# Which earlier transfers a scatter and a fetch wait for at the end of a one-core transformer kernel, and where the last small unit evicts to

## The chip, the cores and the metric

The kernel runs on one core of a Trainium2 chip. The time is that of one execution on the device, in microseconds (us). The kernel before took 2656.06 us as the median of three runs, 2652.81 us the lowest and 2658.04 us the highest.

Engine names: PE is TensorE (PEld its weight loads), DVE is VectorE, ACT is ScalarE, POOL is GpSimd, SP is SyncE. Each works through its own list of instructions in order. Transfers between the on-chip memory and HBM are started by SP (plain loads and stores) or by POOL (all indirect ones here).

## The reference

Two transformer blocks run on 2048 tokens of width 1024. The second ends in a mixture of experts, and this is where the change lies:

```python
best = argmax(sum of the two best scores of each group)   # 4 groups of 4 experts
idx  = top 2 experts inside the best group
gate = the two scores, divided by their sum
y    = sum over the two experts e of gate * ((silu(x @ w_gate[e]) * (x @ w_up[e])) @ w_down[e])
x    = layer_norm(ALPHA * x + y, ln_moe_g, ln_moe_b)
```

So a token gets two contributions, both from experts of one group, and its last layer norm can be done once that group's experts are through.

## The kernel before

The dense parts take the first 2.2 ms and are the same before and after. They leave every token's row in HBM twice: `x3d` (with its gates) to gather from, and `sumd`, already scaled, to which the experts add.

**Units.** The experts' work is cut into units of 256 tokens (n=2, two tiles of 128) or of 128 (n=1, a third tile of an expert that needs one). There are 23 units, with 39 tiles. The last three, to which the text below refers, are: **U3**, expert 14, two tiles; **U2**, expert 14, its third tile; **U1**, expert 15, two tiles. U4 and U5 stand before these. A unit goes through these steps (class `Unit`):

- `gather`: POOL fetches the tokens' rows from `x3d` by index (L1157), one transfer per tile, into a tile of `XG`.
- `transposed`: PE transposes (L240), ACT and DVE split every number into a high and a low part (L171 and L172), and DVE copies the gate (L1334).
- `up(0)`, `up(1)`: the products with gate and up weights (L181), a half at a time; `act(f)`: ACT takes a tanh (L1205), DVE multiplies (L1206, L1207), ACT and DVE split (L171, L172). A unit with n=1 is transposed once more in `turn` (L1217).
- `down`: the product with the down weights (L181), evicted by ACT with the gate as factor (L1231) into a tile `y`, which POOL scatters into `sumd`, adding to what is there (L1232).

**Last norms.** Tokens are listed by group in 18 tiles of 128: 3, 5, 5 and 3 for the four groups, where the last 3 are the tokens of group 3 without expert 15, and 2 more, called group 4 in the code, for those with expert 15. When a group is done, its tiles are fetched from `sumd` (`fetch`, L1429), their mean and variance taken (`measure`, L1444 and L1445 on DVE, or L1439 and L1440 on ACT; the root on POOL, L190 and L192), normed (`norms`, L1450 and L1451 on DVE) and scattered to the output (L1452).

**Order.** `run` writes the units in a software pipeline: while unit i does its up products, unit i-1 does its down products and unit i+2 gathers. `mids`, `turn`, `late` and `hooks` hang work of the last norms into unit i: `mids` before up(1), `turn` after act(1), `late` after the down products of unit i-1. The order on ACT and DVE is that of the code; PE, POOL and SP are put in order by a scheduler, except that `queued` fixes the order of POOL's transfers and roots among themselves.

**Waits.** `adds` holds the scatters of the latest unit, `reads` the fetches since then. A scatter waits until all of `adds` and `reads` have landed; a fetch waits until the latest `adds` have landed. POOL works in order, so what stands behind a waiting transfer waits too.

**Tiles.** `YT` holds two tiles `y` of 4 KB; a new one waits until the scatter from the one before it in that place has landed. `XG` holds four gather tiles. `FX` holds three tiles of fetched rows; the last fetches use `XG` and `MRAW`.

In the last unit (`else` of `run`) the order is up(0), the down products of U2, `last` (measure, norms, the fetches of group 3), up(1), act(1), and the down products of U1. After it come group 4's two fetches, and the five norms still open.

A loop for experts with more tiles than planned follows (L1520). In the traced execution it is not entered.

Of the kernel before, what the change touches and what calls it, by code (L numbers as in the profile page):

```python
# [20 lines left out]
D = 1024  # L21
# [28 lines left out]
def model(ctx, tc, A, out, taps=None, nsb=NSB, upto=9):  # L50
# [44 lines left out]
    def partition(mem, *kbs):  # L95
        ends = [sum(kbs[:j + 1]) for j in range(len(kbs))]
        return [ring("", kb, mem[:, int((e - kb) * 256):int(e * 256)]) for kb, e in zip(kbs, ends)]
# [9 lines left out]
    def acc(n=512):  # L107
        return turns["acc"]((128, n))
# [74 lines left out]
    def mm3(o, lh, ll, rh, rl, start, stop):  # L183
        mm(o, lh, rh, start, False)
        mm(o, lh, rl, False, False)
        mm(o, ll, rh, False, stop)
# [917 lines left out]
    def moe():  # L1104
# [3 lines left out]
        MRAW, MT, XG, YT, GAINS, FX = partition(work, MR_KB, 7.75, 16.25, 8, 8, 40 - MR_KB)  # L1108
# [10 lines left out]
        adds, reads, outs = [], [], []  # L1119

        def apart(a, b):
            tc.declare_no_dep(a.ins, b.ins, reason="other tokens")

        def after(a, b):
            tc.add_manual_dep(a.ins, b.ins.name, mybir.DependencyInfo(mybir.DependencyClass.Sync,
                                                                      mybir.DependencyReason.DATA), reason="same tokens")

        line = [[], []]

        def queued(*ds_):  # L1130

            if line[0]:
                for d in ds_:
                    for o in line[1]:
                        tc.add_manual_dep(d.ins, o.ins.name, mybir.DependencyInfo(
                            mybir.DependencyClass.NoSync, mybir.DependencyReason.DATA), reason="order")
            line[1] = ds_
            return ds_[0]

        class Unit:  # L1140
# [3 lines left out]
            def __init__(self, load, src_gu, src_d, gate, n, lo=DVE, of=None):  # L1144
                self.lo = lo
                self.of = of
                self.load, self.src_gu, self.src_d, self.gate, self.n = load, src_gu, src_d, gate, n
                self.t, self.a = [], {}
                self.gu, self.dw = (of.gu, of.dw) if of else ([], [])

            def gather(self):
# [68 lines left out]
            def down(self):  # L1220
                new = []
                for r in range(self.n):
                    rs = slice(r * 128, (r + 1) * 128)
                    y = YT((128, D))
                    for hf in range(2):
                        hs = slice(hf * 512, (hf + 1) * 512)
                        a = acc()
                        for f in range(2):
                            h, l = self.dw[f]
                            mm3(a, self.th[:, f, rs], self.tl[:, f, rs], h[:, hs], l[:, hs], f == 0, f == 1)  # L1230
                        ACT.activation(y[:, hs], a, AF.Copy, scale=self.gc[r])  # L1231
                    d = POOL.indirect_dma_start(out=sumd[:, :], out_offset=self.at[r], in_=y, in_offset=None,  # L1232
                                                compute_op=OP.add)
                    for o in new:
                        apart(d, o)
                    for o in adds + reads:
                        after(d, o)
                    new.append(d)
                queued(*new)
                adds[:] = new  # L1240
                reads.clear()

        def run(units, early=None, mids={}, turn={}, late={}, hooks={}):
            n = len(units)
            for j in range(min(2, n)):
                units[j].gather()
            units[0].weights_up(range(4))
            units[0].transposed()
            if early:
                early()  # L1250
            if n > 1:
                units[1].weights_up(range(3))
            for i, u in enumerate(units):
                v = units[i + 1] if i + 1 < n else None
                w = units[i + 2] if i + 2 < n else None
                if w:
                    w.gather()
                u.up(0)
                if i:
                    units[i - 1].weights_down(1)  # L1260
                u.weights_down(0)
                u.act(0)
                if i:
                    units[i - 1].turn()
                if not v:
                    if i:
                        units[i - 1].down()
                    u.weights_down(1)
                if i in mids:
                    mids[i]()  # L1270
                u.up(1)
                u.act(1)
                if v:
                    v.transposed()
                    v.weights_up([3])
                    if i in turn:
                        turn[i]()
                    if i:
                        units[i - 1].down()
                    if i in late:  # L1280
                        late[i]()
                    if w:
                        w.weights_up(range(3))
                    for hook in hooks.get(i, ()):
                        hook()
                else:
                    u.turn()
                    u.down()

# [78 lines left out]
        tabgi = tab[:, 80:80 + NL * 16].bitcast(I32)  # L1368
# [55 lines left out]
            DVE.tensor_copy(tabgi, tabg)  # L1424
            POOL.dma_start(tabgd, tabgi)

        def fetch(at, mem):
            x = mem((128, D))
            d = POOL.indirect_dma_start(out=x, out_offset=None, in_=sumd[:, :], in_offset=at)  # L1429
            for o in adds:  # L1430
                after(d, o)
            reads.append(queued(d))
            return x, at

# [14 lines left out]
        def scaled(x, at, mean, op, r, static=True):  # L1449
            DVE.scalar_tensor_tensor(x, x, mean, gains[:, 0], op0=op, op1=OP.mult)  # L1450
            DVE.scalar_tensor_tensor(x, x, r, gains[:, 1], op0=OP.mult, op1=OP.add)  # L1451
            d = POOL.indirect_dma_start(out=out[:, :], out_offset=at, in_=x, in_offset=None,  # L1452
                                        bounds_check=S - 1, oob_is_err=False)
            for o in outs:
                (apart if static else after)(d, o)
            outs.append(d)
            if static:
                queued(d)
# [6 lines left out]
        ready, got, measured = [], [], []  # L1465

        def group_done(g):
            for c in range(NFIN[g]):
                ready.append(bass.IndirectOffsetOnAxis(ap=tabgi[:, g * 16 + c:g * 16 + c + 1], axis=0))

        def measure():
            while got:
                x, at = got.pop(0)
                measured.append((x, at, *stats(x, DVE)))

        def fetches(n, mem=FX):
            for _ in range(min(n, len(ready))):
                got.append(fetch(ready.pop(0), mem))

        def norms():  # L1480
            while measured:
                scaled(*measured.pop(0))

        units, mids, turn, late, hooks = [], {}, {}, {}, {}
        for e in range(16):
            units.append(static(e, 0, 2))
            if e in (4, 8, 12):
                hooks[len(units) - 1] = [lambda e=e: group_done((e - 1) // 4)]
            if BLOCKS[e] == 3:
                units.append(static(e, 2, 1, units[-1]))  # L1490
# [8 lines left out]

        def last():  # L1500
            measure()
            norms()
            group_done(3)
            fetches(NFIN[3], XG)

        mids[len(units) - 1] = last
        with tc.manual_schedule(engines={getattr(mybir.EngineType, e) for e in MANUAL}):
            line[0] = True
            run(units, None, mids, turn, late, hooks)
            line[0] = False  # L1510
            assert not ready
            group_done(4)
            fetches(NFIN[4], MRAW)
# [6 lines left out]
        with tc.For_i(0, nit) as j:  # L1520
            u = overflow(j)
            run([u])
            finish([fetch(u.at[0], FX)], static=False)
            cv = SP.value_load(ov["gown"][0:1, 1, ds(j, 1)], min_val=0, max_val=NL * 16 - 1)
            ix = sml([128, 1], "ix", I32, bufs=5)
            SP.dma_start(ix, tabgd[:, ds(cv, 1)])
            finish([fetch(bass.IndirectOffsetOnAxis(ap=ix, axis=0), FX)], static=False)
# [12 lines left out]
    if upto >= 4:  # L1540
        moe()
# [87 lines left out]
```

## Time and profile before

| what | us |
|---|---|
| median of three runs | 2656.06 |
| the profiled execution | 2657.26 |
| its span, from the first instruction to the last | 2655.5 |
| PE busy in the span | 2522.8 (95%) |
| DVE busy | 1603.0 (60%) |
| ACT busy | 1119.3 (42%) |
| POOL busy | 565.2 (21%) |
| PE busy from 2300 to 2500 us, the middle of the experts | 197.43 of 200.00 |
| PE busy from 2617.35 us to the end | 0.00 of 38.15 |

All times in the rows below are us from the start of the span. A row of the timeline is one instruction, or a run of like instructions of one engine: its start, its duration, the engine, the line, the operation, what it writes and reads, the shapes and the count; in brackets the idle time of that engine before it and what ended it. For an indirect transfer on POOL the duration is that of starting it, not of moving the data. A row of the waits gives who waited for whom, the total in us, how often, and the longest.

### The profile page before, as it was taken

Reading aid. Unit: us, or ns where it says so; the run is one execution under the profiler, and the core shown is the slowest. Engines: PE = TensorE matmul, PEld = TensorE weight load, DVE = VectorE, ACT = ScalarE, POOL = GpSimd, SP = SyncE. Lnnn points to the kernel's source line nnn. Section 1 sums busy time; section 2 is a strip of 40 time slices with the busy share of each in tenths; the row PEclk is TensorE's granted clock in tenths of the full one; section 3 lists DMA queues with packets and bytes.
Section 4 is the critical chain, followed back from the end, with each engine's and each line's share of the span. In section 5 each row is a group of like instructions: output and inputs, shape, how many; then the busy total and the mean of one; then the engine's idle time right before and its main releaser. Section 6 shows DMA issues by size and latency. Waiting matters only on the chain. (4 is left out here: it accounts for less than half of the span.)

```text
span 2655.5 us, 36764 instructions
## 1 busy us (share of the span) xinstructions
PE 2522.8 (95%) x13870; PEld 2139.3 (81%) x13870; DVE 1603.0 (60%) x3223; ACT 1119.3 (42%) x1994; POOL 565.2 (21%) x616
## 2 busy tenths in 40 slices
PE   8899999999999999999999999999999996999993
PEld 8777888888788888878788878787888786999892
DVE  5536357667563667664646666654476656686774
ACT  5644453343343532433445323344443332555552
POOL 0102202221021032110210411012012222344544
PEclk9999999999999999999999999999999997999996
DMA  8861362345313515442244245412422445799985
GB/s 302 298 222 56 100 199 68 122 141 197 96 57 99 187 48 182 139 155 72 88 150 128 72 163 176 138 48 80 157 82 94 153 149 208 220 281 283 263 246 135
DMA packets 122708, 402.04 MB, mean 151 GB/s; under 512 B 15136, under 2 KB 15280, under 8 KB 122528
## 3 DMA queue, kind: packets, MB, share of 16 engines
q1 hardware_dynamic: 105872, 340.30, 37.8%
q0 software_dynamic: 16656, 59.37, 8.5%
q8 instruction: 109, 1.79, 0.3%
q14 instruction: 71, 0.58, 0.1%
HBM read 320.11 MB, written 80.55 MB: 151 GB/s over the span
## 5 line engine op out<-in xcount | busy, mean ns | idle before, releaser
L181 PE MATMUL bank<-rounded 128*128 128x512 f32 (+2 forms) x10628 | 2175.8, 362 | 36.5 <-ACT rounded L171 25.2
L181 PEld LDWEIGHTS bank<-rounded 128*128 128x128 f32 x10628 | 1761.6, 190 | 337.6 <-ACT rounded L171 29.4
L172 DVE TENSOR_TENSOR rounded<-work,rounded 128x1024 fp32r<-128x1024 f32 (+2 forms) x530 | 580.6, 1108 | 462.7 <-ACT rounded L171 408.0
L171 ACT CAST rounded<-work 128x1024 fp32r<-128x1024 f32 (+3 forms) x552 | 510.7, 941 | 658.4 <-PE bank L181 256.4
L171 ACT CAST rounded<-bank 128x512 fp32r<-128x512 f32 (+1 forms) x220 | 112.3, 554 | 221.4 <-PE bank L240 100.9
L181 PE MATMUL bank<-work 128*128 128x128 f32 (+5 forms) x944 | 163.6, 301 | 6.7 <-DVE work L545 2.1
L181 PEld LDWEIGHTS bank<-work 128*128 128x128 f32 (+1 forms) x944 | 130.7, 190 | 36.5 <-issue 5.1
L172 DVE TENSOR_TENSOR rounded<-bank,rounded 128x512 fp32r<-128x512 f32 (+1 forms) x220 | 133.3, 640 | 41.9 <-ACT rounded L171 40.2
L240 PE MATMUL bank<-ident,work 128*128 128x128 f32 x616 | 86.5, 288 | 27.0 <-DMA work<-x3d,tabi 9.3
L240 PEld LDWEIGHTS bank<-ident,work 128*128 128x128 f32 x616 | 73.1, 148 | 40.9 <-DMA work<-x3d,tabi 11.0
L190 POOL TENSOR_SCALAR lnrv<-lnmv 128x1 f32<-128x1 f32 x32 | 40.5, 1266 | 298.5 <-DVE lnmv L692 298.3
L1232 POOL DMA_INDIRECT sumd<-work,tabi x39 | 67.0, 1717 | 148.5 <-ACT work L1231 59.2
L375 POOL TENSOR_SCALAR work<-work 128x512 f32<-128x512 f32 x32 | 25.3, 790 | 342.0 <-ACT work L374 342.0
L685 DVE SCALAR_TENSOR_TENSOR work<-work,bank 128x512 f32<-128x512 f32 x64 | 43.6, 685 | 63.6 <-PE bank L181 63.3
L774 DVE SCALAR_TENSOR_TENSOR work<-work,c_convT 128x512 f32<-128x512 f32 x96 | 72.0, 750 | 2.5 <-ACT work L772 0.7
L1231 ACT ACTIVATE work<-bank,gr 128x512 f32<-128x512 f32 x78 | 52.1, 698 | 46.4 <-DMA sumd<-work,tabi 26.9
L879 POOL TENSOR_TENSOR work<-work 128x512 f32<-128x512 f32 (+6 forms) x40 | 46.1, 1152 | 111.7 <-ACT work L871 109.8
L815 POOL TENSOR_TENSOR work<-work,ar 128x520 f32<-128x520 f32 x16 | 17.0, 1060 | 221.3 <-DVE work L777 170.8
L190 POOL TENSOR_SCALAR rrmsv<-ssq 128x1 f32<-128x1 f32 x34 | 8.8, 258 | 253.4 <-DVE ssq L590 173.4
L926 POOL TENSOR_SCALAR work<-work,xrv 128x256 f32<-128x256 f32 x64 | 31.2, 500 | 141.2 <-DVE xrv L924 141.2
L1157 POOL DMA_INDIRECT work<-x3d,tabi x39 | 53.0, 1360 | 34.8 <-DVE gr L1334 15.8
L583 ACT COPY work<-bank 128x512 f32<-128x512 f32 x32 | 18.7, 586 | 85.2 <-PE bank L181 85.2
(326 smaller groups left out, 2145.8 us busy)
## 6 DMA issues: line engine op xcount, KB each, us to landing
work<-in_w_gu SPq DMA_DIRECT2D x64, 512.0 KB
work<-in_x SPq DMA_DIRECT2D x32, 512.0 KB
work<-in_w_out SPq DMA_DIRECT2D x32, 512.0 KB
work<-wmp SPq DMA_DIRECT2D x32, 512.0 KB
work<-wxa SPq DMA_DIRECT2D x32, 512.0 KB
work<-wvw SPq DMA_DIRECT2D x32, 512.0 KB
work<-in_w_dn SPq DMA_DIRECT2D x32, 512.0 KB
sumd<-work SPq DMA_DIRECT2D x19, 512.0 KB
```

Source lines behind the costliest of these rows:

```text
L171: ACT.copy(hi, src)
L172: return (lo_eng or DVE).tensor_sub(lo, src, f32(hi))
L181: PE.matmul(o, l, r, start=start, stop=stop)
L190: POOL.tensor_scalar(v, src, scale, eps, op0=OP.mult, op1=OP.add)
L240: PE.transpose(p[:, k * 128:(k + 1) * 128], src[:, (4 * hf + k) * 128:(4 * hf + k + 1) * 128], ident)
L685: DVE.scalar_tensor_tensor(oh_, xr, ALPHA, a, op0=OP.mult, op1=OP.add)
L774: DVE.scalar_tensor_tensor(s, z[:, k:k + T], conv[:, k, c:c + 1], s, op0=OP.mult, op1=OP.add)
L879: POOL.tensor_tensor(nx[:, lo:], cur[:, lo:], cur[:, lo - d_:15 + T - d_], op=OP.add)
L926: POOL.tensor_scalar(P[:, h, :], P[:, h, :], rv[:, h:h + 1], 0.0, op0=OP.mult, op1=OP.add)
L1157: queued(POOL.indirect_dma_start(out=xg, out_offset=None, in_=x3d[:, :], in_offset=at))
L1231: ACT.activation(y[:, hs], a, AF.Copy, scale=self.gc[r])
L1232: d = POOL.indirect_dma_start(out=sumd[:, :], out_offset=self.at[r], in_=y, in_offset=None, compute_op=OP.add)
```

## The change

- **Scatters.** A scatter waits for the scatters of the unit before it and no longer for the fetches (inside the written-out part; in the loop it still does). `reads` is not cleared, since only the loop uses it.
- **Fetches.** `group_done` stores the scatters that were the latest when the group ended. A fetch of that group waits for these, not for the latest at its own time.
- **The last unit but one** (U2) evicts into a tile of `XG` in place of `YT`.
- **Norms of the last unit.** In the last unit the norms (two DVE passes and the output scatter) move from before up(1) to behind act(1), on POOL behind the three fetches of group 3; the measuring stays.

```diff
-                self.t, self.a = [], {}
+                self.t, self.a, self.ymem = [], {}, YT
...
-                    y = YT((128, D))
+                    y = self.ymem((128, D))
...
-                    for o in adds + reads:
+                    for o in adds:
                         after(d, o)
+                    for o in reads:
+                        (apart if line[0] else after)(d, o)
                     new.append(d)
                 queued(*new)
                 adds[:] = new
-                reads.clear()
...
                 else:
+                    if i in late:
+                        late[i]()
                     u.turn()
                     u.down()
...
-        def fetch(at, mem):
+        def fetch(at, mem, done=None):
...
+            for o in done or adds:
+                after(d, o)
             for o in adds:
-                after(d, o)
+                if done and o not in done:
+                    apart(d, o)
...
-                ready.append(bass.IndirectOffsetOnAxis(...))
+                ready.append((bass.IndirectOffsetOnAxis(...), tuple(adds)))
...
-                got.append(fetch(ready.pop(0), mem))
+                at, done = ready.pop(0)
+                got.append(fetch(at, mem, done))
...
         def last():
             measure()
-            norms()
             group_done(3)
             fetches(NFIN[3], XG)

-        mids[len(units) - 1] = last
+        mids[len(units) - 1], late[len(units) - 1] = last, norms
+        units[-2].ymem = XG
```

The lines of the changed kernel stand a few further down: L1429 becomes L1433, L1439 and L1440 become L1446 and L1447, L1444 and L1445 become L1451 and L1452, L1450 and L1451 become L1457 and L1458, and L1452 becomes L1459.

On POOL, from U2's scatter to U1's two, before (DMASW0 to DMASW7 are the counters by which POOL's transfers tell that they landed, in rotation: U2's scatter, the first row, counts on 3, the output scatter behind it on 4, the three fetches on 5 to 7):

```order
L1232 DMA sumd<-work,tabi 2432x1024 [waits DMASW1_49,DMASW3_49,DMASW0_49,Activation_49]
L190 TENSOR_SCALAR frv_16946<-fmv_16938 128x1 [waits DVE_49]
L192 TENSOR_TENSOR fr_16950<-frv_16946,mhalf 128x1 [waits Pool_49]
L1452 DMA out_dram<-work,tab 2048x1024 [waits DVE_49]
L1429 DMA work<-sumd,tab 128x1024 [waits DMASW3_49,PE_49]
L1429 DMA work<-sumd,tab 128x1024 [waits DMASW6_49,PE_49]
L1429 DMA work<-sumd,tab 128x1024 [waits PE_49]
L190 TENSOR_SCALAR frv_16947<-fmv_16939 128x1 [waits DVE_49]
L192 TENSOR_TENSOR fr_16951<-frv_16947,mhalf 128x1 [waits Pool_49]
L1232 DMA sumd<-work,tabi 2432x1024 [waits DMASW6_49,DMASW7_49,DMASW5_49,Activation_49]
L1232 DMA sumd<-work,tabi 2432x1024 [waits Activation_49]
```

And now (U2's scatter again counts on 3, the fetches on 4 to 6, the output scatter on 7):

```order
L1232 DMA sumd<-work,tabi 2432x1024 [waits DMASW1_49,DMASW3_49,DMASW0_49,Activation_49]
L190 TENSOR_SCALAR frv_16946<-fmv_16938 128x1 [waits DVE_49]
L192 TENSOR_TENSOR fr_16950<-frv_16946,mhalf 128x1 [waits Pool_49]
L1433 DMA work<-sumd,tab 128x1024 [waits DMASW4_49,DMASW3_49,PE_49]
L1433 DMA work<-sumd,tab 128x1024 [waits PE_49]
L1433 DMA work<-sumd,tab 128x1024 [waits DMASW6_49,PE_49]
L1459 DMA out_dram<-work,tab 2048x1024 [waits DMASW7_49,DVE_49]
L1232 DMA sumd<-work,tabi 2432x1024 [waits Activation_49] x2
L190 TENSOR_SCALAR frv_16947<-fmv_16939 128x1 [waits DVE_49]
```

The output scatter moved behind the three fetches; U1's two scatters wait for their evictions on ACT alone, and the root for a fetched tile, which needs that tile to have landed, moved behind them.

On DVE, in the last unit before U1's second activation (bank_65 holds the up products of the second half):

```order
L172 TENSOR_TENSOR rounded<-work,rounded 128x1024
L1444 BN_STATS fst_16941<-work 128x6 x2
L1445 BN_AGGR fmv_16938<-fst_16941 128x2
L1450 SCALAR_TENSOR_TENSOR work<-work,fmv_16938 128x1024
L1451 SCALAR_TENSOR_TENSOR work<-work,fr_16950 128x1024
L1206 SCALAR_TENSOR_TENSOR work<-work,bank_65 128x256
L1207 TENSOR_TENSOR work<-work,bank_65 128x256
L172 TENSOR_TENSOR rounded<-work,rounded 128x256
```

And now:

```order
L172 TENSOR_TENSOR rounded<-work,rounded 128x1024
L1451 BN_STATS fst_16941<-work 128x6 x2
L1452 BN_AGGR fmv_16938<-fst_16941 128x2
L1206 SCALAR_TENSOR_TENSOR work<-work,bank_65 128x256
L1207 TENSOR_TENSOR work<-work,bank_65 128x256
L172 TENSOR_TENSOR rounded<-work,rounded 128x256
L1457 SCALAR_TENSOR_TENSOR work<-work,fmv_16938 128x1024
L1458 SCALAR_TENSOR_TENSOR work<-work,fr_16950 128x1024
```

The two passes of the norm moved behind the activation. On ACT no instruction moves.

At the very end, on POOL behind group 4's two fetches, before:

```order
L1452 DMA out_dram<-work,tab 2048x1024 [waits DVE_49] x2
L190 TENSOR_SCALAR frv_16947<-fmv_16939 128x1 [waits Activation_49]
L192 TENSOR_TENSOR fr_16951<-frv_16947,mhalf 128x1 [waits Pool_49]
L190 TENSOR_SCALAR frv_16948<-fmv_16940 128x1 [waits DVE_49]
L192 TENSOR_TENSOR fr_16952<-frv_16948,mhalf 128x1 [waits Pool_49]
```

And now:

```order
L1459 DMA out_dram<-work,tab 2048x1024 [waits DMASW4_49,DVE_49]
L1459 DMA out_dram<-work,tab 2048x1024 [waits DMASW5_49,DVE_49]
L190 TENSOR_SCALAR frv_16947<-fmv_16939 128x1 [waits Activation_49,Pool_49]
L1459 DMA out_dram<-work,tab 2048x1024 [waits DMASW6_49,DVE_49]
L192 TENSOR_TENSOR fr_16951<-frv_16947,mhalf 128x1 [waits Pool_49]
L190 TENSOR_SCALAR frv_16948<-fmv_16940 128x1 [waits DVE_49]
L192 TENSOR_TENSOR fr_16952<-frv_16948,mhalf 128x1 [waits Pool_49]
```

One output scatter that stood earlier now stands between the two steps of a root.

## Rows read from the trace of the kernel before

**Rows 1.** Waits from 2240 to 2656 us: us, times, longest; PE, ACT, POOL.

```profile
PE bank L181 <- ACT rounded L171: 7.8, 2, 7.0
PE bank L240 <- DMA work<-x3d,tabi: 3.6, 3, 3.2
...
ACT work L1231 <- DMA sumd<-work,tabi: 26.9, 8, 7.7
...
POOL work L1429 <- DMA sumd<-work,tabi: 25.0, 8, 5.8
POOL sumd L1232 <- DMA work<-sumd,tab: 24.1, 5, 7.4
```

**Rows 2.** Timeline of PE, the last unit.

```profile
2594.90 3.31 PE L181 MATMUL bank<-rounded 128*128 128x256 f32 x13
...
2611.86 5.49 PE L181 MATMUL bank<-rounded 128*128 128x512 f32 x12 [6.95 <-ACT rounded L171]
```

**Rows 3.** Timeline of ACT and DVE, the last unit.

```profile
2602.34 1.27 ACT L1231 ACTIVATE work<-bank,gr 128x512 f32<-128x512 f32 x2 [7.07 <-DMA sumd<-work,tabi]
...
2604.58 1.23 DVE L172 TENSOR_TENSOR rounded<-work,rounded 128x1024 fp32r<-128x1024 f32 x1 [8.79 <-ACT rounded L171]
2605.72 1.28 DVE L1444 BATCH_NORM_STATS2 fst<-work 128x6 f32<-128x512 f32 x2
...
2607.28 1.29 DVE L1450 SCALAR_TENSOR_TENSOR work<-work,fmv 128x1024 f32<-128x1024 f32 x1
...
2610.50 0.41 DVE L1206 SCALAR_TENSOR_TENSOR work<-work,bank 128x256 f32<-128x256 f32 x1
```

**Rows 4.** Timeline of POOL, from 2586 us to the end.

```profile
2586.12 0.57 POOL L192 TENSOR_TENSOR fr<-frv,mhalf 128x1 f32<-128x1 f32 x1
2590.99 1.04 POOL L1429 DMA_INDIRECT work<-sumd,tab  x1 [4.30 <-issue]
2595.93 1.61 POOL L1232 DMA_INDIRECT sumd<-work,tabi  x1 [3.91 <-ACT rounded L171]
2597.84 1.57 POOL L1232 DMA_INDIRECT sumd<-work,tabi  x1 [0.31 <-issue]
...
2605.54 1.69 POOL L1232 DMA_INDIRECT sumd<-work,tabi  x1 [4.80 <-ACT work L1205]
2607.34 1.28 POOL L190 TENSOR_SCALAR frv<-fmv 128x1 f32<-128x1 f32 x1
...
2612.61 1.02 POOL L1429 DMA_INDIRECT work<-sumd,tab  x1 [0.69 <-issue]
...
2615.19 0.94 POOL L1429 DMA_INDIRECT work<-sumd,tab  x1 [0.30 <-issue]
...
2621.31 2.06 POOL L1232 DMA_INDIRECT sumd<-work,tabi  x1 [0.76 <-DMA work<-sumd,tab]
...
2631.38 1.05 POOL L1429 DMA_INDIRECT work<-sumd,tab  x1 [1.60 <-issue]
...
2646.65 0.98 POOL L1452 DMA_INDIRECT out_dram<-work,tab  x1 [0.30 <-POOLq L1520]
```

**Rows 5.** Timeline around the longest wait for a gather, three engines.

```profile
2493.20 1.62 POOL L1232 DMA_INDIRECT sumd<-work,tabi  x1 [6.41 <-ACT work L1231]
...
2501.44 1.26 ACT L1231 ACTIVATE work<-bank,gr 128x512 f32<-128x512 f32 x2 [7.74 <-DMA sumd<-work,tabi]
...
2512.24 1.66 POOL L1157 DMA_INDIRECT work<-x3d,tabi  x1 [0.30 <-issue]
...
2520.76 1.09 PE L240 MATMUL bank<-ident,work 128*128 128x128 f32 x8 [3.19 <-DMA work<-x3d,tabi]
```

**Rows 6.** Busy time by stretch, with the clock granted to PE.

```profile
core 0: us, PE busy (x) PEld busy (x) DVE busy (x) ACT busy (x) POOL busy (x), PEclk, DMA share, GB/s
...
2522.07:2525.48 3.41, 3.41 (x12) 3.08 (x13) 3.34 (x10) 2.45 (x4) 0.74 (x1) 0.50 1.03 259
...
2611.86:2617.35 5.49, 5.49 (x12) 3.81 (x12) 0.76 (x2) 2.06 (x3) 2.98 (x4) 0.50 0.59 176
```

More of the change, by code (lines that the diff above doesn't have):

```diff
@@ L1468, in group_done @@
             for c in range(NFIN[g]):
-                ready.append(bass.IndirectOffsetOnAxis(ap=tabgi[:, g * 16 + c:g * 16 + c + 1], axis=0))
+                ready.append((bass.IndirectOffsetOnAxis(ap=tabgi[:, g * 16 + c:g * 16 + c + 1], axis=0), tuple(adds)))
         def measure():
```

## The prediction

> **What bounds the kernel now.** I read the busy times first, in the table above: PE is busy in 95% of the span, and in the middle of the experts in 197.4 of 200 us, so anything won on another engine there is won only where PE stood still. The waits of the expert stage say where that was [rows 1]: 7.8 us for ACT's rounding, of which 7.0 are one wait, and 3.6 us for gathered rows, nearly all in one wait of 3.2. ACT and POOL wait far more, 26.9 us for scatters that free a tile `y`, 25.0 us of fetches waiting for scatters and 24.1 us of scatters waiting for fetches. The last two feed each other: scatter, fetch and scatter follow one another landing by landing. Off PE's path this is free as long as the tile comes free in time.
>
> At the end it is not free. PE's last wait, 6.95 us, ends at 2611.86, and after PE's last product (2617.35) come 38.15 us without any. The chain of the page names only the last output scatter, so I follow POOL's own timeline [rows 4] backwards: last output scatter 2646.65, group 4's first fetch 2631.38, U1's first scatter 2621.31, last fetch of group 3 2615.19, first one 2612.61, U2's scatter 2605.54. Each but the first waits for the landing of the one before or stands behind it. The end moves by as much as these starts move, and by as much as PE reaches U2 earlier.
>
> **Step 1, U2's scatter: 5.0 us earlier.** Before, it needs two things. Its eviction started at 2602.34, after 7.07 us for a scatter [rows 3], and ended at 2603.61. And U3's second scatter, started at 2597.84, had to land: U3's first took from 2595.93 [rows 4] to 2602.34 [rows 3], 6.4 us, so the second landed at about 2604.2. Add some 0.7 us between a landing and a start, as the last fetch of group 3 shows below. U3's scatters in turn stood behind a fetch at 2590.99 and waited 3.91 us for its landing, and that fetch waited for U4's scatter.
>
> Now U2's products end at 2598.21 [rows 2]; its tile of `XG` held rows that were transposed a unit earlier, so ACT evicts at once, 1.27 us, and is done at 2599.6. The fetch may start behind the root that ended at 2586.69, at 2587.0, if nothing else holds it, and at 2590.99 if something does. U3's first scatter follows after 1.04 and 0.30 us, the second 1.9 us later (2595.93 to 2597.84): 2590.2 to 2594.2. With 6.4 and 0.7 us U2's scatter could go at 2597.3 to 2601.3, and with its eviction at 2599.9 to 2601.3. That is 4.2 to 5.6 us before 2605.54; I take 5.0, near the middle, since nothing shows which end holds.
>
> The row of that fetch bears on it: its 4.30 us of idle time were ended by nothing the profile shows, and at 2607.34 a root's first step of one number per token took 1.28 us [rows 4], as long as the DVE pass started at 2607.28 beside it, 1.29 us [rows 3]. [...]
>
> The tile of `XG` alone is worth little: with the old one ACT would wait for U3's first scatter, now landed at 2594.7 to 2598.7, which is hidden behind PE or costs some tenths. That tile pays only if U3's scatters stay late.
>
> **Step 2, U1's scatters: 3.5 us more.** From U2's scatter to the first fetch 7.07 us passed and to the last 2.58 more [rows 4]; these stay. From the last fetch to U1's first scatter it was 6.12 us, the landing of three fetches. Now an output scatter stands between instead: 0.94 + 0.30 + about 1.0 + 0.30 = 2.6, so 3.5 less. Together U1's first scatter starts at about 2612.8. In return the scatter starts while the fetches still move in POOL's one queue; if its data must wait for theirs, up to 2 us come back, so 1.5 to 3.5. I take 3.5, as the second scatter starts 1.9 us later still and group 4's fetch waits for the later of the two.
>
> Does PE allow it? Before, DVE was held: it waited 8.79 us for ACT's rounding (2604.58), then took the statistics, the norm's first pass at 2607.28 and its second, and only then L1206 at 2610.50, 1.36 us before PE [rows 3]. Now ACT rounds the weights right behind its eviction (2599.6 to 2600.6), DVE needs 1.23 for the low part, 1.28 and 0.2 for the statistics, and reaches L1206 at 2603.3, PE at 2604.7 in place of 2611.86. PE's first half is finished at about that time, so it hardly stops. [...]
>
> **Step 3, the five open norms: 0.5 us lost.** From group 4's fetch to the last output scatter it was 15.27 us [rows 4]. On POOL one output scatter, about 1.0 + 0.3 us, now stands between the two steps of a root; on DVE both first passes come ahead of both second ones. I take half of the lesser, 0.5 lost, and bound it by one pass of 1.29 us either way.
>
> **Step 4, the experts before: 3.5 us earlier.** PE waited 3.19 us for gathered rows, until 2520.76 [rows 5], and ran the next 3.41 us at a granted clock of 0.50 [rows 6], which loses 1.7: 4.9 in all. That gather was started at 2512.24, behind scatters delayed by the pattern above: the one at 2493.20 had waited 6.41 us, and ACT then 7.74 for it [rows 5]. Without the waits for fetches these scatters leave earlier and the gather finds a queue less full. It still starts when its tile is free, at about the same time, so I don't count the whole wait: 2.0 of 3.19 and 1.5 of the clock. The bounds are 4.9 and, if a new wait of this size appears elsewhere, -4.9. PE's other waits there total about 3 us and do not hang on scatters.
>
> **Sum.** 5.0 + 3.5 - 0.5 + 3.5 = 11.5 us. The profiled execution took 2657.26 us (span 2655.5, 1.8 around it), 1.2 above the median of the three runs. 2657.26 - 11.5 = 2645.8. The bounds add up to between 4.2 + 1.5 - 1.3 - 4.9 = -0.5 (slower by half a us) and 5.6 + 3.5 + 1.3 + 4.9 = 15.3.
>
> **The rivals.**
> - *PE gives nothing before the end.* The gather still comes late, since its start is bound to its tile and other weights move at the same time. Steps 1 to 3 stay: 8.0, so 2649.3. For it: the gather took 8.5 us with POOL busy starting other transfers around it. Against: only this one of 39 gathers made PE wait so long.
> - *The fetch at 2590.99 does not move, and the scatters share the queue with the fetches.* Steps 1 and 2 at their low ends, step 3 at its own, step 4 nothing: 4.2 + 1.5 - 1.3 = 4.4, so 2652.9, which is no change by a measurement.
> - *Slower: gathers land late.* POOL no longer pauses between a fetch and the scatter behind it, so gathers stand in the queue behind more data. A gather started at 2512.24 and needed by PE 5.3 us later already misses by 3.19. Each such miss costs 4.9 with the clock. One eats step 4's gain and more; the end's 8.0 are gone with two, and by the third the kernel is slower: 2657.3 - 8.0 + 14.7 = 2664.0. Against it: the order of POOL's transfers before the last unit is the same, and each scatter leaves earlier or at the same time, so a gather has less before it, not more.
> - *The change does not do what it says.* Were the removed waits implied by others, the order would still show them: U1's scatters had three landings in their list and now have ACT alone. I give this nothing of its own.
>
> **How the numbers follow.** Forecast (both PE's and POOL's part) 0.52; nothing before the end 0.22; the low ends 0.13; slower 0.05; and 0.08 for more than the forecast, as 2640, with all terms at their upper ends. A measurement of this kernel can tell about 0.2%, 5.3 us: below 2650.7 it is faster. The forecast, the first rival and the upper case lie there, the low ends inside 5.3: faster 0.82, same 0.13, slower 0.05. The range goes from 2639.5, near the upper end of all terms less the run's 1.2, to 2652.5, just short of the low ends: that leaves out the slower case and most of the low one.
>
> **What would show it.** In the profile after: U2's eviction with no wait for a scatter, and its scatter 6 to 8 us behind U3's second; PE's last wait under 1 us and the last products at a clock of 1.00; U1's scatters about 2.6 us behind group 3's last fetch; some 15 to 17 us from group 4's first fetch to the last output scatter; 24.1 us of scatters waiting for fetches gone; no wait of 3 us for a gather. Wrong would be a PE wait of several us that was not there, U3's scatters still around 2596 relative to the same PE work, or U1's scatters waiting for ACT.

## The result and the profile after

The changed kernel took 2640.91 us (median of 6 runs, 2633.84 to 2644.51), the one before 2656.83 (6 runs, 2652.81 to 2658.04): a ratio of 0.994 with the interval 0.9925 to 0.9955, or 15.9 us less (12.0 to 19.9). The forecast was 2645.8, 11.5 us less: the direction and the range held, the gain was larger. The profiled execution took 2640.2 us, its span is 2638.5, 17.0 less than before's.

The waits of the expert stage, 2240 us to the end (what waited, for what: us in all, times, longest):

```profile
POOL sumd L1232 <- ACT work L1231: 108.9, 30, 13.5
...
POOL work L1433 <- DMA sumd<-work,tabi: 5.6, 2, 5.1
...
PE bank L240 <- DVE rounded L172: 2.5, 2, 1.5
...
PE bank L181 <- ACT rounded L171: 0.8, 1, 0.8
```

Against [rows 1], ACT's 26.9 us for scatters and POOL's 24.1 us of scatters waiting for fetches are gone, the fetches' waits put down to scatters are 5.6 us in place of 25.0, and PE waits for no gather and has no wait of 7 us. POOL now idles for evictions, the work that its scatters really need.

POOL's tail, the counterpart of [rows 4]:

```profile
2575.55 1.04 POOL L1433 DMA_INDIRECT work<-sumd,tab  x1 [0.20 <-issue]
2576.90 1.61 POOL L1232 DMA_INDIRECT sumd<-work,tabi  x1 [0.30 <-issue]
2579.34 1.84 POOL L1232 DMA_INDIRECT sumd<-work,tabi  x1 [0.84 <-ACT work L1231]
...
2590.07 1.55 POOL L1232 DMA_INDIRECT sumd<-work,tabi  x1 [6.91 <-ACT work L1231]
...
2593.80 0.57 POOL L192 TENSOR_TENSOR fr<-frv,mhalf 128x1 f32<-128x1 f32 x1
2597.06 1.70 POOL L1433 DMA_INDIRECT work<-sumd,tab  x1 [2.70 <-PE bank L181]
2599.07 0.97 POOL L1433 DMA_INDIRECT work<-sumd,tab  x1 [0.30 <-issue]
2600.34 0.94 POOL L1433 DMA_INDIRECT work<-sumd,tab  x1 [0.30 <-issue]
2601.58 1.00 POOL L1459 DMA_INDIRECT out_dram<-work,tab  x1 [0.30 <-issue]
2602.89 1.59 POOL L1232 DMA_INDIRECT sumd<-work,tabi  x1 [0.30 <-issue]
...
2614.01 1.51 POOL L1433 DMA_INDIRECT work<-sumd,tab  x1 [1.40 <-issue]
...
2630.01 0.97 POOL L1459 DMA_INDIRECT out_dram<-work,tab  x1 [0.30 <-issue]
```

U3's two scatters (2576.90, 2579.34) stand right behind the fetch; U2's (2590.07) waits 6.91 us for its own eviction and nothing else; U1's first (2602.89) is 2.55 us behind group 3's last fetch, where it was 6.12. The fetch at 2597.06 is put down to PE, which had long left that tile; what it really waited for is U2's scatter, started 6.99 us earlier, whose landing this trace has at 2596.28.

PE, ACT and DVE in the last unit (against [rows 2, 3]), and the last stretch of PE with its clock (the seventh figure behind the stretch, after the busy times; against [rows 6]):

```profile
2583.88 0.38 PE L1217 MATMUL bank<-ident,work 128*128 128x128 f32 x2
2584.02 14.54 PE L181 MATMUL bank<-rounded 128*128 128x256 f32 x84
```

```profile
2587.95 0.69 ACT L1231 ACTIVATE work<-bank,gr 128x512 f32<-128x512 f32 x1 [1.81 <-PE bank L181]
2589.10 0.69 ACT L1231 ACTIVATE work<-bank,gr 128x512 f32<-128x512 f32 x1 [0.46 <-PE bank L181]
...
2598.65 0.69 ACT L1231 ACTIVATE work<-bank,gr 128x512 f32<-128x512 f32 x1 [0.69 <-PEq L1528]
```

```profile
2593.47 0.42 DVE L1206 SCALAR_TENSOR_TENSOR work<-work,bank 128x256 f32<-128x256 f32 x1
...
2596.55 1.28 DVE L1458 SCALAR_TENSOR_TENSOR work<-work,fr 128x1024 f32<-128x1024 f32 x1
```

```profile
2592.00:2598.56 6.56, 6.56 (x33) 5.03 (x31) 5.13 (x8) 2.85 (x5) 2.26 (x3) 1.00 0.50 80
```

PE runs its last 84 products without a stop, the last 6.56 us of them at a granted clock of 1.00, where the last 5.49 us before had 0.50 [rows 6]. U2's first half is evicted while PE still makes the second, so only 0.69 us of eviction lies behind the last product in place of 1.27.

The middle of the experts is where the forecast was furthest off. Before, POOL's rows ahead of the gather of [rows 5]:

```profile
2485.50 1.29 POOL L1429 DMA_INDIRECT work<-sumd,tab  x1 [0.92 <-DMA sumd<-work,tabi]
2493.20 1.62 POOL L1232 DMA_INDIRECT sumd<-work,tabi  x1 [6.41 <-ACT work L1231]
...
2501.61 1.03 POOL L1429 DMA_INDIRECT work<-sumd,tab  x1 [1.87 <-DMA sumd<-work,tabi]
2507.11 1.61 POOL L1232 DMA_INDIRECT sumd<-work,tabi  x1 [4.47 <-ACT rounded L171]
2509.03 1.57 POOL L1232 DMA_INDIRECT sumd<-work,tabi  x1 [0.30 <-issue]
2510.91 1.03 POOL L1452 DMA_INDIRECT out_dram<-work,tab  x1 [0.30 <-issue]
```

and PE's turn in front of it, and the next one's:

```profile
2502.06 0.38 PE L1217 MATMUL bank<-ident,work 128*128 128x128 f32 x2
...
2535.83 0.38 PE L1217 MATMUL bank<-ident,work 128*128 128x128 f32 x2
```

The same place after, POOL and then PE:

```profile
2481.39 1.63 POOL L1232 DMA_INDIRECT sumd<-work,tabi  x1 [4.45 <-ACT work L1231]
...
2490.55 1.03 POOL L1433 DMA_INDIRECT work<-sumd,tab  x1 [0.19 <-issue]
2491.89 1.61 POOL L1232 DMA_INDIRECT sumd<-work,tabi  x1 [0.30 <-issue]
2494.33 1.86 POOL L1232 DMA_INDIRECT sumd<-work,tabi  x1 [0.83 <-ACT work L1231]
2496.61 1.59 POOL L1459 DMA_INDIRECT out_dram<-work,tab  x1 [0.41 <-DVE work L1458]
2498.50 1.00 POOL L1157 DMA_INDIRECT work<-x3d,tabi  x1 [0.30 <-issue]
```

```profile
2498.87 0.38 PE L1217 MATMUL bank<-ident,work 128*128 128x128 f32 x2
...
2514.22 1.91 PE L240 MATMUL bank<-ident,work 128*128 128x128 f32 x16
...
2527.19 0.38 PE L1217 MATMUL bank<-ident,work 128*128 128x128 f32 x2
```

Before, the gather started 10.18 us behind the turn (2512.24 - 2502.06), after 0.37 us ahead of it (2498.50): 10.55 us earlier by PE's own work. From turn to turn PE took 33.77 us and now 28.32. The order isn't the reason: the first 101 of POOL's 114 indirect transfers, up to U2's scatter, stand in the same order in both traces.

Both traces set side by side by PE's own landmarks, in us, with the forecast's terms. The first stretch ends where PE waits for ACT's rounding, at 2347.21 before, and holds the dense parts. The last turn is counted here and below from the second of its two products, 0.11 us behind the start of its row (2593.12 and 2583.99):

| stretch | before | after | gained | forecast |
|---|---|---|---|---|
| start to that wait | 2347.21 | 2344.84 | 2.4 | 0 |
| to the last turn (step 4) | 245.91 | 239.15 | 6.8 | 3.5 |
| last turn to U2's scatter (step 1) | 12.42 | 6.08 | 6.3 | 5.0 |
| U2's to U1's first scatter (step 2) | 15.77 | 12.82 | 3.0 | 3.5 |
| U1's to group 4's first fetch (step 2) | 10.07 | 11.12 | -1.1 | 0 |
| to the last output scatter (step 3) | 15.27 | 16.00 | -0.7 | -0.5 |
| to the end | 8.90 | 8.44 | 0.5 | 0 |

The first row is no effect of the change: the first fetch, ahead of which no wait differs, starts at 2327.51 before and at 2325.18 after, so 2.3 of the 2.4 us are there already. In the fourteen traces of this study the row lay between 2342.35 and 2351.04. The rest sums to 14.7.

### The profile page after: what moved, and what is told of

Same layout as the page of the kernel before. It is cut to its first block, busy times and chain, and to the rows that moved or that the text cites. A ratio compares the mean times of both kernels' runs of the same rounds, so it can differ in the third digit from the quotient of the medians.

```text
span 2638.5 us, 36773 instructions
## 1 busy us (share of the span) xinstructions
PE 2514.9 (95%) x13870; PEld 2133.7 (81%) x13870; DVE 1602.1 (61%) x3223; ACT 1119.9 (42%) x1994; POOL 572.0 (22%) x616
## 4 chain that ended last, share of the span: by engine, by line
PE 75%; DVE 8%; ACT 4%; DMA 3%; POOL 3%; issue 2%; ACTq 0%; POOLq 0%; SPq 0%; DVEq 0%
PE bank L181 70%; DVE rounded L172 3%; PE bank L240 2%; ACT rounded L171 2%; DMA work<-wxa 1%; DMA sumd<-work,tabi 1%; PE bank L488 1%; DVE work L695 1%; POOL lnrv L190 1%; PE bank L932 1%; ACT work L511 0%; POOL lnr L192 0%; PE bank L806 0%; DVE lnst L686 0%; DVE work L685 0%
## 5 line engine op out<-in xcount | busy, mean ns | idle before, releaser
L172 DVE TENSOR_TENSOR rounded<-work,rounded 128x1024 fp32r<-128x1024 f32 (+2 forms) x530 | 580.2, 1108 | 449.4 <-ACT rounded L171 405.8
L172 DVE TENSOR_TENSOR rounded<-bank,rounded 128x512 fp32r<-128x512 f32 (+1 forms) x220 | 133.2, 640 | 42.7 <-ACT rounded L171 41.3
L190 POOL TENSOR_SCALAR lnrv<-lnmv 128x1 f32<-128x1 f32 x32 | 40.6, 1267 | 297.3 <-DVE lnmv L692 297.1
L1157 POOL DMA_INDIRECT work<-x3d,tabi x39 | 57.7, 1479 | 34.9 <-DVE gr L1337 15.9
L190 POOL TENSOR_SCALAR rrmsv<-ssq 128x1 f32<-128x1 f32 x34 | 9.4, 277 | 256.2 <-DVE ssq L590 173.7
```

Source lines behind the costliest of these rows:

```text
L172: return (lo_eng or DVE).tensor_sub(lo, src, f32(hi))
L190: POOL.tensor_scalar(v, src, scale, eps, op0=OP.mult, op1=OP.add)
L1157: queued(POOL.indirect_dma_start(out=xg, out_offset=None, in_=x3d[:, :], in_offset=at))
```

## The experiments

Twelve runs were made, in three groups of four, each group beside the kernel before (medians 2655.0, 2655.38 and 2656.41 us). Two of them repeat a kernel unchanged. The table has, from each trace in us, PE's waits for gathers in all, its last wait if one stands behind the last turn, and two stretches; then the median time and the ratio on record, which can differ from the quotient of the medians by some 0.0006.

| kernel | gather waits of PE | PE's last wait | last turn to U2's scatter | last turn to end | time, us | ratio to before |
|---|---|---|---|---|---|---|
| before | 3.60 | 6.95 | 12.42 | 62.43 | 2656.83 | 1 |
| e1_before_again | 3.00 | 5.55 | 11.02 | 61.04 | 2653.84 | 1.0002 (0.9989 to 1.0014) |
| e2_scatters_alone | 0 | 2.34 | 6.14 | 55.49 | 2640.66 | 0.9947 (0.993 to 0.9964) |
| e3_fetches_alone | 0.83 | 5.05 | 10.50 | 60.69 | 2650.12 | 0.9984 (0.9972 to 0.9997) |
| e4_waits_alone | 0 | 2.34 | 6.11 | 55.16 | 2642.76 | 0.9957 (0.9942 to 0.9973) |
| e5_waits_kept | 3.05 | none | 13.66 | 65.47 | 2656.4 | 1.0001 (0.9989 to 1.0012) |
| e6_yt_kept | 0 | none | 6.14 | 54.52 | 2639.77 | 0.9942 (0.9924 to 0.996) |
| e7_norms_first | 0 | 2.29 | 6.07 | 55.22 | 2641.16 | 0.9947 (0.993 to 0.9964) |
| e8_scatters_first | 0 | none | 6.08 | 55.73 | 2643.72 | 0.9959 (0.9943 to 0.9976) |
| e9_middle_alone | 0 | 2.34 | 7.72 | 57.76 | 2644.77 | 0.9962 (0.9947 to 0.9976) |
| e10_end_alone | 4.16 | 4.34 | 10.33 | 57.58 | 2651.97 | 0.9981 (0.997 to 0.9992) |
| e11_scatters_first_ordered | 0 | none | 6.06 | 55.17 | 2644.09 | 0.9958 (0.9946 to 0.9971) |
| after | 0 | none | 6.08 | 54.46 | 2640.91 | 0.994 (0.9925 to 0.9955) |
| e12_after_again | 0 | none | 6.08 | 54.22 | 2640.78 | 0.9935 (0.9921 to 0.995) |

**e1_before_again**, the kernel before, unchanged, to see which of its waits recur.

> The kernel before, unchanged, with a second profile. Theory A (the wait of 3.19 us for gathered rows at 2520 belongs to the pattern of waits): a wait of 2 to 4 us for gathered rows stands at the same place again, and PE reaches U2's transposes (L1217) at 2590 to 2595. Rival B (it was chance in one execution): no such wait here, L1217 some 5 us earlier relative to PE's work at 2345. Either way 2656 within 3.

The long wait for a gather recurs, at another gather:

```profile
2574.33 3.22 PE L240 MATMUL bank<-ident,work 128*128 128x128 f32 x16 [2.83 <-DMA work<-x3d,tabi]
```

So it belongs to the kernel and not to one gather: POOL is late in places that can shift with the execution (in e5 and e10 below the wait is back near before's place).

**e2_scatters_alone**, the kernel before with only the scatters' edit.

```diff
-                    for o in adds + reads:
+                    for o in adds:
+                    for o in reads:
+                        (apart if line[0] else after)(d, o)
-                reads.clear()
```

> Before, with the scatters' wait for the fetches taken out and nothing else. Theory A (the scatters' wait carries most, since it delays U3's scatters and U1's): about 8 us faster, 2648, with U1's scatters some 3 us behind group 3's last fetch. Rival C (the fetches' wait for the latest scatters carries as much, since scatters stand behind them on POOL anyway): 4 us or less, 2652.

The expectation missed: this edit alone brings 14.1 us (9.6 to 18.6), all that can be told of the gain. The fetches' wait, which I took for half of a pair, need not be cut: fetches still wait in this trace, 11.5 us put down to scatters in place of 25.0, but PE waits for no gather.

**e3_fetches_alone**, the changed kernel with the old wait of the scatters, the old place of the norms and the old tile.

```diff
-                    for o in adds:
-                    for o in reads:
-                        (apart if line[0] else after)(d, o)
+                    for o in adds + reads:
+                reads.clear()
-        mids[len(units) - 1], late[len(units) - 1] = last, norms
-        units[-2].ymem = XG
+        mids[len(units) - 1] = last
```

(and `norms()` back in `last`)

> Before, with only the fetches' wait narrowed to their own group's scatters. Theory A: U3's scatters leave about 4 us earlier, U1's gain nothing, 4 to 5 us faster, 2651.5. Rival C: 8 us or more, 2648 or less.

4.2 us, with the interval 0.8 to 7.4, as expected. The other half alone helps a little; a scatter behind a fetch still waits for its landing (one wait of 7.5 us is put down to a fetch, five of 24.1 in all before).

**e4_waits_alone**, both waits changed, norms and tile as before.

```diff
-        mids[len(units) - 1], late[len(units) - 1] = last, norms
-        units[-2].ymem = XG
+        mids[len(units) - 1] = last
```

> Both narrowed waits, but U2 evicts to the old tiles and the last unit's norms stay before up(1). Theory A (the tile and the norms' place are covered): the time of the changed kernel, 2641 within 2. Rival D (they are worth what PE's end gained by them): 3 to 6 us slower than that, 2645 or more, with U1's scatters waiting for ACT.

The same as e2 within the measurement, and 55.16 to 55.49 in the trace from the last turn on.

**e5_waits_kept**, the kernel before with the tile of `XG` and the moved norms, and the old waits.

```diff
+        mids[len(units) - 1], late[len(units) - 1] = last, norms
+        units[-2].ymem = XG
```

> The old waits, with U2's tile of XG and the norms behind act(1). Theory A, as the runs so far have it (the waits are the gain, the other two edits hide under the landing chain): PE's last wait falls from 5.6 or 7 us to under 2 and PE ends some 8 us earlier, but U2's scatter still waits for U3's and U1's for three fetches, so the time gains 0 to 3 us only, 2653. Rival D (PE's late end is the bound): 6 us or more, 2649 or less.

Nothing gained, although PE's last wait of 7 us is gone, the largest wait of the stage on the engine that is busy 95% of the time. PE stops less at the end and POOL is no earlier; in this trace it even takes 3.0 us more from the last turn to the end (65.47 against 62.43), for which no run shows the cause. POOL's fetch and scatters of U3 and its scatter of U2, ACT's last part of U2's eviction, and PE's gather:

```profile
2593.15 1.04 POOL L1431 DMA_INDIRECT work<-sumd,tab  x1 [4.39 <-issue]
2598.22 1.61 POOL L1232 DMA_INDIRECT sumd<-work,tabi  x1 [4.04 <-DMA work<-sumd,tab]
2600.14 1.57 POOL L1232 DMA_INDIRECT sumd<-work,tabi  x1 [0.31 <-issue]
...
2608.07 1.56 POOL L1232 DMA_INDIRECT sumd<-work,tabi  x1 [4.74 <-ACT work L1231]
```

```profile
2599.55 0.69 ACT L1231 ACTIVATE work<-bank,gr 128x512 f32<-128x512 f32 x1 [0.47 <-PE bank L181]
```

```profile
2522.16 3.24 PE L240 MATMUL bank<-ident,work 128*128 128x128 f32 x16 [3.05 <-DMA work<-x3d,tabi]
```

ACT, which the row of U2's scatter names, was done with U2's eviction at 2600.24, 7.8 us ahead of it: U2's scatter starts 7.93 us behind U3's second and waits for that one's landing, as in [rows 4].

**e6_yt_kept**, the changed kernel without the tile of `XG`.

```diff
-        units[-2].ymem = XG
```

> The changed kernel with U2's eviction back in the old tiles. Theory A: no wait of ACT for a scatter in the last unit, since U3's scatters now land before U2's products end; the time of the changed kernel within 1 us, 2641. Rival D: a wait of 2 us or more there, and as much in the time.

The same time, and 6.14 us from the turn to U2's scatter against 6.08. The tile is worth nothing that these times can tell.

**e7_norms_first**, the changed kernel with the norms back before the fetches.

```diff
-        mids[len(units) - 1], late[len(units) - 1] = last, norms
+        mids[len(units) - 1] = last
```

(and `norms()` back in `last`)

> The changed kernel with the last unit's norms back before up(1). From the run with the waits alone: a PE wait of 2.3 us appears and the first fetch stands 8.35 us behind U2's scatter in place of 7.0, U1's scatters 1.24 in place of 2.55 behind the last fetch, so 0.7 to 1 us in the time, 2641.7. Rival D: 3 us or more.

PE waits 2.29 us again, and the first fetch comes 8.36 us behind U2's scatter in place of 6.99; but the output scatter is then already out and the three fetches take 2.59 us in place of 3.28, so that U1's first scatter comes even 0.6 us earlier by PE's last turn. Later 1.4 us go between group 4's fetch and the last output scatter (17.38 in place of 16.00). At the end the traces differ by 0.8 us, less than the times can tell.

**e8_scatters_first**, the changed kernel with group 3's fetches behind U1's scatters.

```diff
             group_done(3)
-            fetches(NFIN[3], XG)
...
             run(units, None, mids, turn, late, hooks)
+            fetches(NFIN[3], XG)
```

> The changed kernel with group 3's three fetches moved behind U1's two scatters. Theory A (POOL's order is what holds U1's scatters, which are evicted by 2599.4 and started at 2602.9 and 2604.8): they start some 4.5 us earlier, group 4's first fetch 5 to 7 us earlier, but five tiles are then normed in one go, at least 17 us of DVE work behind the first landing, so 3 to 5 us faster than the changed kernel, 2637. Rival E (the queue is the bound: three fetches and two scatters move the same bytes in either order): within 1 us, 2641.

POOL and DVE at its end:

```profile
2596.99 1.55 POOL L1232 DMA_INDIRECT sumd<-work,tabi  x1 [0.30 <-ACT work L1231]
2598.84 1.57 POOL L1232 DMA_INDIRECT sumd<-work,tabi  x1 [0.30 <-issue]
...
2600.72 1.01 POOL L1433 DMA_INDIRECT work<-sumd,tab  x1 [0.30 <-issue]
...
2606.64 0.94 POOL L1433 DMA_INDIRECT work<-sumd,tab  x1 [2.39 <-DMA sumd<-work,tabi]
```

```profile
2608.32 1.29 DVE L1451 BATCH_NORM_STATS2 fst<-work 128x6 f32<-128x512 f32 x2 [12.97 <-DMA work<-sumd,tab]
```

The 3 to 5 us expected did not come. Group 4's first fetch comes 4.9 us earlier by PE's last turn, but the first of the five open norms starts at 2608.32, 1.7 us behind it, where in the changed kernel three of them had had their first pass by then. From that fetch to the last output scatter it takes 22.46 us in place of 16.00, 6.5 more. What was won on one branch was lost on the other.

**e9_middle_alone** and **e10_end_alone**: e2, with the old wait for the fetches kept in the last three units (e9), or in all but the last three (e10). `fresh` holds the fetches since the latest unit's scatters, and `free` is true where a unit isn't named in the loop.

```diff
+                    for o in reads:
+                        (apart if line[0] and (self.free or o not in fresh) else after)(d, o)
...
+        for u in units[-3:]:      # e10: units[:-3]
+            u.free = False
```

> Before, with the scatters' wait for the fetches taken out in all units but the last three. Theory F (the gain has two parts: gathers in the middle, 5 to 7 us up to U2's transposes, and the landing chain at the end, 8 to 9 us): L1217 comes within 1 us of the changed kernel's, counted from PE's wait at 2345, and the chain behind it keeps the times of before; 5 to 6 us faster, 2649.5. Rival G (the middle does nothing for the time, its waits are chance): same as before, 2655.

> Before, with the scatters' wait for the fetches taken out in the last three units only. Theory F: a wait of 2 to 4 us for gathered rows stands somewhere between 2480 and 2590, and from L1217 to the end it takes the 55.5 us of the run with the scatters alone in place of 62.4; 7 to 9 us faster, 2647.5. Rival G: all of the gain, 2641.

10.1 us (6.4 to 14.1) and 5.0 us (2.1 to 8.0), together the 15 of the whole. By the expectations it was to be 5 to 6 and 7 to 9. I had put the parting line in the wrong place: with U4's scatter free, U3's fetch and scatters come earlier even if U3's own wait is kept (7.72 us from turn to U2's scatter), and with it bound, the end's first step is worth 2.1 us and not 6.3 (10.33). e10 keeps its gather waits:

```profile
2523.38 3.67 PE L240 MATMUL bank<-ident,work 128*128 128x128 f32 x16 [2.77 <-DMA work<-x3d,tabi]
```

**e11_scatters_first_ordered**: e8, with the five last norms in a written order, each tile's two passes together, DVE and ACT in turns.

```diff
+            st, on = {}, (DVE, ACT, DVE, ACT, DVE)
+            for k in (0, 1, 2):
+                st[k] = stats(got[k][0], on[k])
+            for k in range(5):
+                scaled(*got[k], *st[k])
+                if k < 2:
+                    st[k + 3] = stats(got[k + 3][0], on[k + 3])
```

> The changed kernel with group 3's fetches behind U1's scatters and the five last norms in a fixed order on DVE and ACT (each tile's two passes together). Theory A: what the first try of that order gained on POOL (group 4's first fetch 7 us earlier) and lost in the norms (22.46 in place of 16.00 us) is partly kept: from L1217 to the end 52 to 53.5 us in place of 54.5, so 1 to 2.5 us faster than the changed kernel, 2639. Rival E: no gain, 54 or more.

0.6 us shorter in the trace than e8 and no faster in time: the order of the passes isn't what held e8 back.

**e12_after_again**, the changed kernel once more.

> The changed kernel once more with a second profile. Theory F: again no wait for gathered rows over 0.5 us behind 2240, and 54.5 us within 0.5 from L1217 to the end; 2641. Rival G: a wait of 2 to 4 us for gathered rows appears here too.

The stretches of after behind PE's first landmark repeat to 0.3 us, and again no gather makes PE wait. Over all fourteen traces: the nine in which the middle's scatters don't wait for fetches have no wait of PE for a gather, the five in which they do (before, e1, e3, e5, e10) have 0.83 to 4.16 us. From PE's first landmark to the last turn the nine take 239.14 to 239.16 us, the five 240.41 to 247.78. No version beats the changed kernel by more than the measurement tells.

## Why the prediction was right, and where its sizes were wrong

**What bounds the kernel** was read rightly: scatter and fetch waiting for each other's landings set the end, and PE's place in it. The prediction priced the two waits as one pair; e2 against e4 shows that cutting the scatters' wait is enough.

**Step 4 is the step that failed.** It said of the gather: "It still starts when its tile is free, at about the same time, so I don't count the whole wait". The tile was not what it waited for. `XG` turns through four tiles, and the last reads of the two that were to be filled, PE's transposes (by 2490.2) and DVE's copies of the gates (by 2497.0), had ended 15 us earlier; the gather's own row [rows 5] shows 0.30 us of idle time, the distance of one transfer behind another on POOL. What held it stood in the rows above it, in the same queue: two scatters, each behind a fetch that had to land, with waits of 6.41 us (2493.20) and 4.47 us (2507.11). The profile puts the first down to ACT, but ACT's eviction for it had ended at 2483.47; after, its counterpart (2481.39) leaves 0.3 us behind the eviction. With these waits gone, the gather starts 10.55 us earlier and the standstill goes whole: 3.60 us of waits and about 1.7 for the clock (an estimate: half of the 3.41 us at 0.50 [rows 6]), and some 1.5 whose cause I didn't trace, 0.8 of them between the turns at 2472.93 and 2502.06 (29.13 us against 28.29): 6.8 against 3.5 and against a bound of 4.9, which had counted one wait and its clock alone. By e9 and e10 the middle carries some two thirds of the gain in time, 10.1 of 15, with intervals of several us on each; part of that is the end's first step, which starts in the middle.

**Step 1** was mis-sized, 6.3 us against 5.0 and a bound of 5.6. U3's scatters came earlier than either end I had given (U2's follows 10.7 us behind the second, and I had said 6 to 8), because the fetch in front of them starts 8.44 us ahead of the last turn (2575.55) where it was 2.13 (2590.99), and the earliest start that I had allowed was 6.1 ahead (2587.0). So U2's own eviction decides, as the upper bound said; and that eviction has 0.69 us left behind the last product and not 1.27, since its first half is done beside PE. 5.6 + 0.6 makes 6.2 of the 6.3. The low case, that the fetch at 2590.99 does not move, fell: the fetch starts 0.20 us behind its root (2575.55), and in e5, which keeps the old wait, it stands 4.39 us again. "Issue" in its row of [rows 4], with 4.30 us, hid the wait for a transfer's landing.

**Step 2** came out at 1.9 in all: 3.0 for U1's scatters, less 1.1 given back behind them. The fetches follow U2's scatter at 6.99 us as foreseen (7.07), but the three take 3.28 in place of 2.58: the moved norm's second pass on DVE (2596.55 to 2597.83) lies beside the first of them, which takes 1.70 us and not 1.02. The give-back was foreseen at up to 2, should data have to wait for that of the fetches; that cause was not shown, but the times of e8 agree with it: from U1's second scatter to group 4's first fetch, which waits for its landing, it takes 9.2 us in the changed kernel, with the three fetches started just ahead, and 7.8 in e8, where they stand behind (7.7 before). PE did what was said: it doesn't stop, ends 14.57 us behind its last turn in place of 24.23 (9.7 earlier), and U1's last eviction (2599.34) has 3.55 us to spare before the first scatter (2602.89). That the PE gain is worth nothing by itself is e5; that the moved norms cost and bring next to nothing is e7; that the tile of `XG` is "worth little" is e6.

**Step 3** was 0.7 lost, forecast 0.5.

**The rivals.** "PE gives nothing before the end" (2649.3) and "the fetch does not move" (2652.9) fell by the rows above. "Gathers land late" fell most clearly: gathers have less before them, not more, and PE waits for none. The time is that of the upper case (2640), given 0.08, but partly by luck: its terms were not all at their upper ends. Steps 1 and 4 went past theirs by 0.7 and 1.9 us, steps 2 and 3 stayed 1.6 and 2.0 short, and 2.4 of the 17.0 us between the two traces are the dense part's.

Open stays why the dense part takes up to 8.7 us more in some executions; no experiment touched it. Between the two traces of the changed kernel, whose spans differ by 1.5 us, it is all of the difference (2344.84 and 2346.58).

## What to carry to other kernels

When an instruction starts right behind the one before it on its engine (the gather of [rows 5], 0.30 us), look for what delayed the rows above it; follow the queue back before saying that its start is bound by its data. Here the false waits between POOL's transfers were paid by what stood behind them too: without them the gather started 10.55 us earlier, and PE's 3.60 us of waits for gathers were gone. So the price of such a wait can't be read off its own rows alone, and cutting one side of such a pair was enough here (e2, 14.1 us). In e5 PE's largest wait, 6.95 us, was gone without a gain (2656.4 us), as POOL's chain set the end.

## What the runs showed of the hardware

In the changed kernel's trace a gather that POOL started while DVE ran a pass over 128x1024 (L172 from `work` and `rounded`) had a longer row, which ended some 0.9 us behind that pass. One of them, and the four passes on DVE, the third of which starts at 2485.12 and ends at 2486.33:

```profile
2485.26 1.94 POOL L1157 DMA_INDIRECT work<-x3d,tabi  x1 [0.31 <-issue]
```

```profile
2482.85 4.62 DVE L172 TENSOR_TENSOR rounded<-work,rounded 128x1024 fp32r<-128x1024 f32 x4
```

Of its 38 gathers that could be sorted in this way, the 16 without such a pass at their start took 0.94 to 1.08 us; the 22 started within one took 1.22 to 2.06 us, and less the rest of the pass 0.81 to 0.89 (median 0.87). Their starts were not held by the pass: 20 of the 22 came 0.30 to 0.31 us behind the row before them on POOL. The fetch at 2597.06 fits, beside L1458: DVE's pass ran another 0.77 us, and 1.70 - 0.77 = 0.93.

A root's first step on POOL (L190) in the last norms took 0.18 to 0.20 us without such a pass beside it, also beside DVE's statistics (0.19 at 2606.42). In the ten roots of the two traces that started within one (here also the two passes of a norm, L1450 and L1451 before, L1457 and L1458 after) it ended 0.05 us behind that pass: 1.22 us at 2609.03 in the changed kernel, beside the pass from 2608.91 to 2610.19, and 0.55 at 2625.32 before, where the pass from 2624.54 to 2625.82 was more than half over. So the prediction's reading of the root at 2607.34 holds.
